# A two-stream encoder trunk: two more groups of input columns in the planned weave, new costs in its planner, and the first stream's attention over the columns that are left

## The chip, the core and the metric

The kernel runs on one core of a Trainium2 chip. TensorE (PE) multiplies, with its weight loads (PEld) beside the matmuls; VectorE (DVE) and ScalarE (ACT) do the elementwise work; GpSimd (POOL) does a few memsets; SyncE (SP) issues all DMAs. The metric is the device time of one execution in microseconds; lower is better.

## What is computed

Two requests of 512 tokens with 1024 channels go through the same two layers. Each layer is `x + rmsnorm(branch(rmsnorm(x)))`.

- Layer 0, RWKV-7: projections r, k, v, z (1024 x 1024 each) of the token mixed with its neighbours, small two-stage projections for decay and learning rate, and then, per head of 64 channels and in both directions, the scan `S_t = S_(t-1) (diag(decay_t) + a_t b_t^T) + v_t k_t^T`, `y_t = S_t r_t`. The two directions are summed, normalised per head, given a bonus term, gated with silu(z) and projected by w_o.
- Layer 1, neighbourhood attention: a projection w_in of 1024 x 4096 gives q, k, v, z; 16 heads attend on an 8 x 64 grid of tokens, each token to a window of 8 rows x 16 columns with a learned bias; the output is gated with silu(z) and projected by w_ao.

Everything is float32. A large product is made as three fast products: each operand is split into a rounded part hi (a cast on ACT) and the rest lo (a subtraction on DVE), and hi·hi, hi·lo and lo·hi are summed.

## The kernel before, in words

**Stages.** A prelude (stream 0 and 1: norms, mixing, first columns) runs to about 172 us. Then comes the *weave* (`scan_phase`, line 1585, and `weave`, line 1553), to 1172 us. It holds the scan of both streams, all that prepares and finishes it, and a stream of 76 columns. A column is a piece of a weight matrix of 1024 x 128; its product with the operands of one stream is 24 matmuls of 128 x 128 by 512. Then `rest` (line 1685) runs the attention of stream 0 beside the columns left over (to 1345 us), its output projection `out1(0)`, and the same for stream 1.

**The weave's order is written out by a planner.** Each piece of work is a generator (`Thread`, line 190) that yields the engine of its next operations, a gate, and a time from which its inputs are there. `Clock` (line 51) keeps a modelled time for each engine and each tile: `one` (line 112) gives each emitted instruction a cost on its engine, and what reads its result may start after that cost plus the engine's latency in `LAT`. `weave` picks, again and again, an open thread whose time has come: work for other engines ahead of work for PE, and then the lowest rank. On an engine other than PE nothing is emitted that would start later than its inputs by more than `EPS` (60 ns), or further ahead of PE's time than `AHEADE` (200 ns for ACT and DVE). The instructions of PE, DVE and ACT then stand on their engines in just this order. The ranks: the scan's steps 0, its helpers 0.5 to 1, `preps` 1.5, evacuation of columns (`posts`) 2, operands 2.5, splits of weights 3 or 9, `finish` 4, `inverse` 5, products 9.

**The scan** goes over 8 blocks (two streams x four groups of four heads) of 8 steps. `preps` (917) makes a block's factors. `inverse` (922) inverts 32 triangles per partition with thirty pairs of DVE operations, each reading what the one before wrote (lines 941 and 942), and then some transposes and small products. `step` (1080) passes through PE, ACT, PE, ACT, PE and DVE, where the new state S is an addition (1165) and a multiplication (1166). `finish` (1180) normalises a block's output.

**The columns** (`stream`, 1510; `flow`, 681) come in groups with common operands: nine groups, r, v, k, r, v, z, w_o of stream 0, the last two of z, and w_in of stream 0, of which the weave takes `4 * NPA` = 20 columns. `loads` brings weights on SP, at most three halves ahead (`NRAW`), `splits` splits them, `fetched` brings operand tiles, `operands` splits those into pairs of `act` buffers (18 in all, nine pairs), `products` multiplies.

The last group's operands are the residual x1 = x + h·post0·rstd, times pre1. In `x1n` (1518) and `operands` one thread makes each of the eight tiles k as six operations in turn: scale on DVE (1526), add on DVE (1529), hi on ACT (728), lo on DVE (733), square on ACT (1534), sum on DVE (1538). h is fetched to one of three `xr` buffers, x to a spare `act` or `vs` buffer.

**Attention of stream 0** (`rest`): for each of the last 8 - NPA = 3 groups p of w_in its four columns (`inproj`, 1318, 32 steps a group), then the eight columns of w_o of stream 1 (`out0`, 1264, 64 steps). Beside them the heads run (`heads`, 1348; 16 units for each of eight pairs of heads): `run(g, (a, n))` emits n units per step of g.

```python
for p in range(self.NPA, NP):
    run(self.inproj(0, self.xa, p), (a, self.POST0))
    queue.append(self.heads(0, p))
run(self.out0(1), (a, self.POST))
while queue:
    next(a)
```

With POST0 0.7 and POST 1.0. This stage is ordered by the tile framework's own scheduler, not by `Clock`.

Of the kernel before, what the change touches and what calls it, by code (L numbers as in the profile page):

```python
# [19 lines left out]
P = 128  # L20
T = 512
# [29 lines left out]
class Clock:  # L51
# [1 line left out]


    ENG = {"PE": "P", "Activation": "A", "DVE": "D", "Pool": "G", "SP": "S"}
    LAT = dict(P=200.0, A=45.0, D=45.0, G=90.0, S=0.0)
    BANKS = ("pf", "zy", "us", "pm", "pg", "pt", "po")

    def __init__(self, nc):
# [52 lines left out]
    def one(self, e, i):  # L112
        ap = lambda xs: [x for x in xs if hasattr(x, "bass_ap")]
        outs, ins = ap(i.outs), ap(i.ins)
        if not outs:
            return 0.0
        name = lambda x: x.bass_ap.tensor.name
        t = issued = self.t[e]
        for table, xs in ((self.made, ins), (self.used, outs)):
            for x in xs:  # L120
                for f, at in table.get(name(x), {}).items():
                    if f != e or e == "S":
                        t = max(t, at)
        free = lambda x: int(np.prod([n for _, n in x.ap[1:]])) if len(x.ap) > 1 else 1
        n = max([free(outs[0])] + [free(x) for x in ins[:1]])
        if e == "P":
            t, done = self.matmul(i, ins, free(outs[0]), t)
        elif e == "S":

            self.t[e] = issued = max(issued, self.t["P"]) + 380.0  # L130
            size = outs[0].ap[0][1] * free(outs[0]) * 4
            c = size * 0.0027 + 150.0
            self.dq = max(issued + 800.0, self.dq) + c
            done = max(self.dq, t + 800.0 + c) + 670.0
        else:
            if e == "A":
                c = 175.0 + 0.86 * n
            elif e == "G":
                c = 150.0 + n
            else:  # L140
                kind = type(i).__name__
                sb = [x for x in ins if free(x) > 8 and not name(x).startswith(self.BANKS)]
                c = 80.0 + 1.06 * n
                if "Reciprocal" in kind:
                    c = 80.0 + 6.2 * n
                elif getattr(i, "is_tensor_tensor_scan", False):
                    c = 80.0 + 2.1 * n
                elif "Transpose" in kind:
                    c = 80.0 + 1.8 * n
                elif len(sb) == 1 and len(ins) <= 2 and "TensorTensor" not in kind and "Reduce" not in kind and free(outs[0]) == n:  # L150
                    c = 110.0 + 0.53 * n if not getattr(i, "is_scalar_tensor_tensor", False) else 130.0 + 1.06 * n
            self.t[e] = t + c
            done = t + c + self.LAT[e]
        for x in ins:
            u = self.used.setdefault(name(x), {})
            u[e] = max(u.get(e, 0.0), done)
            self.slot[name(x)] = True
        for x in outs:
            for table in (self.used, self.made):
# [54 lines left out]

class Trunk:
    NACT, NW, NRAW, NXR, NTMP, WP = 18, 4, 3, 3, 5, 512
    POST0, POST, POST2, POST3, NPA = 0.7, 1.0, 0.15, 0.66, 5
    HP, HS = (1000, 0), 1000
    OUT1 = ("pg", "pg", "pg", "pg")
    HPA = 1000  # L220
# [13 lines left out]
    CH, FIRST, WFIRST = 100, 17, 3  # L234
    NVS = 2
    NZ1, STOCK, EPS, NEAR = 6, 1, 60.0, 400.0
    AHEADE = dict(S=3000.0, A=200.0, D=200.0)

    def __init__(self, ctx, tc, a):
# [441 lines left out]
    def flow(self):  # L681
# [2 lines left out]
        nc, did, ck = self.nc, self.did, self.clock  # L684
        cols = [(g, j, src, done) for g, (_, _, c) in enumerate(self.groups) for j, (src, done) in enumerate(c)]
        name = lambda *xs: [x.tensor.name for x in xs]
        raw, w, x, todo = {}, {}, {}, {}
        self.xq, self.post = x, {}
        for k, t in enumerate(self.groups[0][1]):
# [19 lines left out]
        def fetched():  # L709
            for g, (ready, source, _) in enumerate(self.groups):  # L710
                for k in range(KT if g else 0):
                    yield "S", lambda: ready() and 8 * g + k < min(did["x"] + self.NACT // 2 + self.NXR - 1, 8 * len(self.groups) - 8 + did["x1"] + self.NXR)
                    todo[g, k] = source(k)

        def operands():
            for g in range(1, len(self.groups)):
                for k in range(KT):
                    yield "S", lambda: (g, k) in todo
                    src, before, by, then = todo.pop((g, k))
                    for e, f in before:  # L720
                        yield e, None, lambda c: c.at(name(src))
                        f()
                    yield "A", lambda: 8 * g + k < did["x"] + self.NACT // 2 - (by is not None), lambda c: c.at(name(src))
                    lo, hi = self.pair()
                    if by is None:
                        nc.scalar.copy(hi, src)
                    else:
                        nc.scalar.activation(hi, src, AF.Identity, scale=by)
                    yield "D"
                    if by is None:  # L730
                        nc.vector.tensor_tensor(lo, src, hi.bitcast(F32), op=ALU.subtract)  # L731
                    else:
                        nc.vector.scalar_tensor_tensor(lo, src, by, hi.bitcast(F32), op0=ALU.mult, op1=ALU.subtract)
                    x[g, k] = hi, lo
                    for e, f in then:
                        yield e
                        f()

        def products():
            free, room = self.bank()  # L740
# [18 lines left out]
        def posts(a):  # L759
# [5 lines left out]
        few = lambda: did["split"] - did["k"] // 4 <= self.STOCK  # L765
        return [
            Thread(lambda: 0, loads()), Thread(lambda: 3 if few() else 9, splits()), Thread(lambda: 0, fetched()), Thread(lambda: 2.5, operands()),
            Thread(lambda: 9, products()), Thread(lambda: 2, posts(0)), Thread(lambda: 2, posts(1))]


    def prep(self, s, p):
# [139 lines left out]
        ks = kps[0]  # L911
        yield "D"
        vt.tensor_tensor(ks, kps[0], kps[1], op=ALU.add)
        vt.scalar_tensor_tensor(ks, ks, self.vec("rk", p), r, op0=ALU.mult, op1=ALU.mult)
        self.save("ks", s, p, ks)

# [5 lines left out]
    def inverse(self, s, pb):  # L922
# [14 lines left out]
        for q in range(1, 31):  # L937
            n = 31 - q
            tv = tmp[:, :n * q].rearrange("p (i j) -> p i j", i=n)
            yield "D"  # L940
            vt.tensor_tensor(tv, N[:, q + 1:, q:q + 1].broadcast_to([P, n, q]), N[:, q:q + 1, :q].broadcast_to([P, n, q]), op=ALU.mult)  # L941
            vt.tensor_tensor(N[:, q + 1:, :q], tv, N[:, q + 1:, :q], op=ALU.add)  # L942
        yield "D"
        vt.tensor_tensor(N, N, self.lower, op=ALU.mult)
        vt.memset(N.rearrange("p i j -> p (i j)")[:, 0:1024:33], 1.0)

        yield "D"
# [132 lines left out]
    def step(self, q):  # L1080
# [77 lines left out]
        if not st.last:  # L1158
# [4 lines left out]
                vt.tensor_tensor(st.S, so, wc, op=ALU.mult)  # L1163
            else:
                vt.tensor_tensor(st.S, so, before.S, op=ALU.add)
                vt.tensor_tensor(st.S, st.S, wc, op=ALU.mult)

        yi = st.y[:, min(st.i, 7 - st.i)]
# [11 lines left out]
    def finish(self, s, pb, y):  # L1180
# [14 lines left out]
        bc = lambda t: t.unsqueeze(2).broadcast_to([P, 16, HD])  # L1195
        yield "D", None, need(y)
        vt.tensor_reduce(st[:, 0], yv, axis=AX.X, op=ALU.add)
        vt.tensor_scalar(st[:, 1], st[:, 0], -1.0 / HD, None, op0=ALU.mult)
        yield "D"
        vt.tensor_tensor(yv, yv, bc(st[:, 1]), op=ALU.add)  # L1200
# [71 lines left out]
    def norm0(self, s):  # L1272

        nc = self.nc
        if s == 0:
# [1 line left out]
            self.x1_acc = self.t("vs", bufs=self.NVS)  # L1277
            yield from self.rstds(self.h_acc)
            self.made.add(("hr", s))
            yield "P", lambda: self.did["x1"] == KT, lambda c: c.at([self.x1_acc.tensor.name])  # L1280
            yield from self.rstds(self.x1_acc)
            self.x1_rstd = self.x1_acc
            self.made.add(("x1", s))
# [226 lines left out]
    def stream(self):  # L1510
# [1 line left out]
        sp = self.sp  # L1512
        cols = lambda s, kind, ps=range(NP): [
            (self.a["w_" + kind][p], lambda ps, p=p: self.column(s, kind, p, ps)) for p in ps]
        disk = lambda kind, s: lambda k: (self.load(self.t("xr", bufs=self.NXR), sp[kind, s, k]), [], None, [])
        vt, act = self.nc.vector, self.nc.scalar

        def x1n(k):

            h = self.load(self.t("xr", bufs=self.NXR), sp["h", 0, k])  # L1520
            x = self.t("act", (P, T), self.NACT, F32R).bitcast(F32) if k % 3 else self.t("vs", bufs=self.NVS)
            self.load(x, self.a["xc"][0][k * P:(k + 1) * P, :])
            sq = []

            def scaled():
                vt.scalar_tensor_tensor(h, h, self.vec("post0", k), self.h_acc, op0=ALU.mult, op1=ALU.mult)

            def added():
                vt.tensor_tensor(h, h, x, op=ALU.add)
                self.save("x1", 0, k, h)  # L1530

            def squared():
                sq.append(self.tmp() if k else self.x1_acc)
                act.activation(sq[0], h, AF.Square)

            def summed():
                if k:
                    vt.tensor_tensor(self.x1_acc, sq[0], self.x1_acc, op=ALU.add)
                self.did["x1"] += 1

            return h, [("D", scaled), ("D", added)], self.vec("pre1", k), [("A", squared), ("D", summed)]

        now = lambda: True
        groups = [
# [310 lines left out]
```

## Time and profile before

| | us |
|---|---|
| median of 3 runs | 1693.5 (1692.28 to 1696.38) |
| the profiled execution | 1695.69, of it the span 1693.9 |
| PE busy | 1542.3 (91%) |
| DVE busy | 1243.6 (73%) |
| ACT busy | 987.9 (58%) |
| mean granted clock of PE | 0.958 |
| the weave, 172 to 1172 | PE busy 879.4 of 1000 |
| attention of stream 0, 1172 to 1345 | PE busy 173.0 of 173 |

A row of a group reads: line, engine, operation, out<-in, partitions x elements, count | busy us, mean ns of one | idle time of the engine just before them, and who ended it. A row in order of time reads: start, duration, engine, line, and in brackets the idle time before and who ended it. A row of stretches reads: from:to, length, busy us (and instructions) of PE, PEld, DVE, ACT and POOL, the granted clock, the DMA's share and its GB/s; asked for one line, it has only that line's engines.

### The profile page before, as it was taken

The page shows a single profiled execution, that of the slowest core. Times are in us where ns is not written, and L with a number is a line of the kernel's source. Part 1 is how long each engine was busy: PE and PEld are TensorE (multiplying, and loading weights), DVE is VectorE, ACT ScalarE, POOL GpSimd, SP SyncE. Part 2 cuts the span into 40 slices and gives each one's busy share as a digit, 9 for nine tenths or more (in the row PEclk, how much of TensorE's full clock was granted, in tenths as well). Part 3 has the DMA queues.
Part 4 walks back from the last instruction along what each step waited for, and adds up shares of the span by engine and source line. Part 5 has one row for each costly group of instructions (what it writes and reads, how often), then busy time and mean ns, then how long its engine had stood idle before and what let it go on. Part 6 is the DMA issues. An engine that isn't in the chain of part 4 may idle for free.

```text
span 1693.9 us, 45876 instructions
## 1 busy us (share of the span) xinstructions
PE 1542.3 (91%) x18624; PEld 1171.7 (69%) x18624; DVE 1243.6 (73%) x2725; ACT 987.9 (58%) x1979; POOL 24.1 (1%) x94
## 2 busy tenths in 40 slices
PE   7989788889998988889978689999999999999998
PEld 6767556666676766666656477777777887777776
DVE  8985679688786886897878988656566686555564
ACT  5443655767665666667576545544567765555562
POOL 0000000000000000000000000000000000000000
PEclk9989989899999999999989799999999999999999
DMA  5435687786686777885667754557555346545553
GB/s 207 162 124 187 201 286 222 209 257 224 196 258 197 233 230 220 273 262 188 210 226 233 225 181 141 158 169 261 177 184 181 113 138 240 188 155 174 168 175 106
DMA packets 240819, 336.23 MB, mean 198 GB/s; under 512 B 53696, under 2 KB 119360, under 8 KB 240608
## 3 DMA queue, kind: packets, MB, share of 16 engines
q1 hardware_dynamic: 240608, 333.31, 61.2%
q8 instruction: 146, 2.39, 0.6%
q14 instruction: 65, 0.53, 0.1%
HBM read 227.71 MB, written 105.51 MB: 197 GB/s over the span
## 4 chain that ended last, share of the span: by engine, by line
PE 59%; DVE 16%; DMA 9%; ACT 9%; issue 5%; SPq 1%; DVEq 0%; ACTq 0%
PE pg L406 6%; PE pg L407 6%; PE pg L408 6%; PE pm L751 5%; PE pm L752 4%; PE pm L753 4%; PE sc L1375 2%; PE pf L1035 2%; PE po L1408 2%; DVE etmp L941 2%; DVE N L942 2%; PE pt L1393 1%; PE zy L1106 1%; DVE wlo L705 1%; PE us L1133 1%
## 5 line engine op out<-in xcount | busy, mean ns | idle before, releaser
L751 PE MATMUL pm<-act,whi 128*128 128x512 f32 x608 | 272.5, 448 | 19.4 <-ACT whi L703 8.9
L753 PE MATMUL pm<-act,wlo 128*128 128x512 f32 x608 | 249.2, 410 | 13.3 <-DVE wlo L705 11.9
L752 PE MATMUL pm<-act,whi 128*128 128x512 f32 x608 | 248.6, 409 | 11.2 <-DVE act L731 8.3
L406 PE MATMUL pg<-act,whi 128*128 128x512 f32 x480 | 199.8, 417 | 0.0
L407 PE MATMUL pg<-act,whi 128*128 128x512 f32 x480 | 190.2, 396 | 0.0
L408 PE MATMUL pg<-act,wlo 128*128 128x512 f32 x480 | 189.8, 396 | 0.0
L355 ACT CAST whi<-raw 128x512 fp32r<-128x512 f32 x156 | 96.4, 619 | 134.8 <-PE pg L407 87.9
L751 PEld LDWEIGHTS pm<-act,whi 128*128 128x128 f32 x608 | 119.2, 196 | 60.5 <-issue 13.3
L753 PEld LDWEIGHTS pm<-act,wlo 128*128 128x128 f32 x608 | 119.3, 196 | 50.0 <-DVE wlo L705 19.4
L356 DVE TENSOR_TENSOR wlo<-raw,whi 128x512 fp32r<-128x512 f32 x156 | 106.7, 686 | 59.8 <-ACT whi L355 49.8
L752 PEld LDWEIGHTS pm<-act,whi 128*128 128x128 f32 x608 | 119.7, 197 | 34.8 <-DVE act L731 11.4
L705 DVE TENSOR_TENSOR wlo<-raw,whi 128x512 fp32r<-128x512 f32 x152 | 103.3, 684 | 46.8 <-ACT whi L703 43.7
L703 ACT CAST whi<-raw 128x512 fp32r<-128x512 f32 x152 | 93.1, 618 | 31.4 <-PE pm L752 13.1
L408 PEld LDWEIGHTS pg<-act,wlo 128*128 128x128 f32 x480 | 90.7, 189 | 19.9 <-issue 0.7
L406 PEld LDWEIGHTS pg<-act,whi 128*128 128x128 f32 x480 | 90.9, 189 | 19.4 <-issue 4.8
L407 PEld LDWEIGHTS pg<-act,whi 128*128 128x128 f32 x480 | 91.0, 190 | 17.2 <-issue 3.0
L942 DVE TENSOR_TENSOR N<-etmp,N 128x30 f32<-128x30 f32 (+14 forms) x240 | 79.7, 332 | 8.2
L941 DVE TENSOR_TENSOR etmp<-N 128x30 f32<-128x30 f32 (+14 forms) x240 | 78.4, 327 | 4.5
L1386 DVE CUSTOM_DVE_ANT_0 sb<-sc,bias 128x256 f32<-128x256 f32 x128 | 50.5, 420 | 39.8 <-PE pt L1393 29.2
L1389 ACT ACTIVATE sb<-sb,mx 128x256 f32<-128x256 f32 x128 | 64.2, 503 | 16.4 <-DVE mx L1388 16.0
L1035 PE MATMUL pf<-cab 64*64 64x128 f32 (+1 forms) x2048 | 69.9, 274 | 3.7 <-issue 3.1
L1145 ACT COPY X<-us 64x256 f32<-64x256 f32 x128 | 46.8, 366 | 33.7 <-PE zy L1013 31.2
(381 smaller groups left out, 3298.3 us busy)
## 6 DMA issues: line engine op xcount, KB each, us to landing
dab<-ab SPq DMA_DIRECT2D x32, 1024.0 KB, 7.3
cab<-dab SPq DMA_DIRECT2D x64, 512.0 KB, 4.3
raw<-in_w_in_dram SPq DMA_DIRECT2D x128, 256.0 KB, 3.4
bias<-in_rpb_dram SPq DMA_DIRECT2D x32, 384.0 KB, 4.1
raw<-in_w_z_dram SPq DMA_DIRECT2D x32, 256.0 KB, 5.3
dz<-tmp SPq DMA_DIRECT2D x32, 256.0 KB, 3.3
raw<-in_w_k_dram SPq DMA_DIRECT2D x32, 256.0 KB, 2.6
dk<-tmp SPq DMA_DIRECT2D x32, 256.0 KB, 3.1
```

Of the source, the lines that this page charges most:

```text
L355: self.nc.scalar.copy(hi, src)
L356: (eng or self.nc.vector).tensor_tensor(lo, src, hi.bitcast(F32), op=ALU.subtract)
L406: nc.tensor.matmul(ps, hi, x[k][0], start=(k == 0), stop=False)
L407: nc.tensor.matmul(ps, hi, x[k][1], start=False, stop=False)
L408: nc.tensor.matmul(ps, lo, x[k][0], start=False, stop=(k == KT - 1))
L705: nc.vector.tensor_tensor(lo, raw.pop(h), hi.bitcast(F32), op=ALU.subtract)
L751: nc.tensor.matmul(ps, hi[:, at], xh, start=(k == 0), stop=False)
L752: nc.tensor.matmul(ps, hi[:, at], xl, start=False, stop=False)
L753: nc.tensor.matmul(ps, lo[:, at], xh, start=False, stop=(k == KT - 1))
L941: vt.tensor_tensor(tv, N[:, q + 1:, q:q + 1].broadcast_to([P, n, q]), N[:, q:q + 1, :q].broadcast_to([P, n, q]), op=ALU.mult)
L942: vt.tensor_tensor(N[:, q + 1:, :q], tv, N[:, q + 1:, :q], op=ALU.add)
L1035: end = nc.tensor.matmul(st.f[half(a), h, 0, d, g] if st.last else st.f[half(a), h, :, d, g], ab[half(h), d, g, 2 * e[d] + 1 - a], rt if s ...
```

## The change

1. `NPA` goes from 5 to 7: the weave takes 28 columns of w_in, the attention stretch one group of w_in and the eight columns of w_o. `POST0` goes to 1.0 and `POST` to 1.32.
2. The planner's costs: latencies 210, 125, 116 and 120 ns for PE, ACT, DVE and POOL (200, 45, 45, 90 before); ACT 85 + 0.85 n ns (175 + 0.86 n), DVE 82 + 1.02 n (80 + 1.06 n). On ACT and DVE an operation that reads what the same engine wrote now waits for the latency too.
3. The residual is made by three threads of rank 0.6, `residual`, `scaled` and `squares`, instead of within `operands`. `held` counts the `act` buffers in use; the h tiles of k = 3 and 4 (`HACT`) are fetched to `act` buffers. The norm of x1 waits for the last sum (`x1s`).
4. Five more yields between two DVE operations of one thread: in `prep`, `inverse` (twice), `step`, `finish`, so that other work may be put between them.

```diff
-    LAT = dict(P=200.0, A=45.0, D=45.0, G=90.0, S=0.0)
+    LAT = dict(P=210.0, A=125.0, D=116.0, G=120.0, S=0.0)
...
-                    if f != e or e == "S":
+                    if f != e or e == "S" or e in "AD" and table is self.made:
...
-                c = 175.0 + 0.86 * n
+                c = 85.0 + 0.85 * n
...
-                c = 80.0 + 1.06 * n
+                c = 82.0 + 1.02 * n
...
-    POST0, POST, POST2, POST3, NPA = 0.7, 1.0, 0.15, 0.66, 5
+    POST0, POST, POST2, POST3, NPA = 1.0, 1.32, 0.15, 0.66, 7
...
+    HACT = (3, 4)
...
-                    yield "S", lambda: ready() and 8 * g + k < min(did["x"] + self.NACT // 2 + self.NXR - 1, 8 * len(self.groups) - 8 + did["x1"] + self.NXR)
+                    if g < len(self.groups) - 1:
+                        yield "S", lambda: ready() and 8 * g + k < did["x"] + self.NACT // 2 + self.NXR - 1
+                    else:
+                        yield "S", lambda: ready() and k < did["x1"] + 5 and held() + (k in self.HACT) + (k % 3 > 0) <= self.NACT
                     todo[g, k] = source(k)
 
+        def held():
+            return 2 * (8 + did["pair"] - did["x"]) + did["act"]
...
+        def residual():
+            for k in range(KT):
+                yield "S", lambda: (last, k) in todo
+                h, xc = todo[last, k]
+                yield "D", None, lambda c: c.at(name(h))
+                nc.vector.scalar_tensor_tensor(h, h, self.vec("post0", k), self.h_acc, op0=ALU.mult, op1=ALU.mult)
+                yield "D", None, lambda c: c.at(name(h, xc))
+                nc.vector.tensor_tensor(h, h, xc, op=ALU.add)
+                self.save("x1", 0, k, h)
+                did["act"] -= k % 3 > 0
+                did["sum"] += 1
+
+        def scaled():
+            for k in range(KT):
+                yield "S", lambda: did["sum"] > k
+                h = todo[last, k][0]
+                yield "A", lambda: held() + 2 <= self.NACT, lambda c: c.at(name(h))
+                lo, hi = self.pair()
+                did["pair"] += 1
+                nc.scalar.activation(hi, h, AF.Identity, scale=self.vec("pre1", k))
+                yield "D"
+                nc.vector.scalar_tensor_tensor(lo, h, self.vec("pre1", k), hi.bitcast(F32), op0=ALU.mult, op1=ALU.subtract)
+                x[last, k] = hi, lo
+
+        def squares():
+            for k in range(KT):
+                yield "S", lambda: (last, k) in x
+                h = todo.pop((last, k))[0]
+                yield "A", None, lambda c: c.at(name(h))
+                sq = self.tmp() if k else self.x1_acc
+                nc.scalar.activation(sq, h, AF.Square)
+                did["act"] -= k in self.HACT
+                did["x1"] += 1
+                if k:
+                    yield "D"
+                    nc.vector.tensor_tensor(self.x1_acc, sq, self.x1_acc, op=ALU.add)
+                did["x1s"] += 1
...
+            Thread(lambda: 0.6, residual()), Thread(lambda: 0.6, scaled()), Thread(lambda: 0.6, squares()),
...
             vt.tensor_tensor(tv, N[:, q + 1:, q:q + 1].broadcast_to([P, n, q]), N[:, q:q + 1, :q].broadcast_to([P, n, q]), op=ALU.mult)
+            yield "D"
             vt.tensor_tensor(N[:, q + 1:, :q], tv, N[:, q + 1:, :q], op=ALU.add)
...
                 vt.tensor_tensor(st.S, so, before.S, op=ALU.add)
+                yield "D"
                 vt.tensor_tensor(st.S, st.S, wc, op=ALU.mult)
```

More of the change, by code (lines that the diff above doesn't have):

```diff
@@ L686, in flow @@
         name = lambda *xs: [x.tensor.name for x in xs]
+        last = len(self.groups) - 1
         raw, w, x, todo = {}, {}, {}, {}
@@ L713, in fetched @@
                     todo[g, k] = source(k)
+        def held():
+            return 2 * (8 + did["pair"] - did["x"]) + did["act"]
         def operands():
-            for g in range(1, len(self.groups)):
+            for g in range(1, len(self.groups) - 1):
                 for k in range(KT):
                     yield "S", lambda: (g, k) in todo
[L719 to L723, printed above, removed]
+                    src = todo.pop((g, k))
+                    yield "A", lambda: 8 * g + k < did["x"] + self.NACT // 2, lambda c: c.at(name(src))
@@ L724, in operands @@
                     lo, hi = self.pair()
[L725 to L728, printed above, removed]
+                    did["pair"] += 1
+                    nc.scalar.copy(hi, src)
                     yield "D"
[L730 to L733, printed above, removed]
+                    nc.vector.tensor_tensor(lo, src, hi.bitcast(F32), op=ALU.subtract)
@@ L734, in operands @@
                     x[g, k] = hi, lo
-                    for e, f in then:
-                        yield e
-                        f()
+        def residual():
[9 more added lines that the diff above has]
+                did["sum"] += 1
@@ new lines, in scaled @@
+        def scaled():
[4 more added lines that the diff above has]
+                lo, hi = self.pair()
+                did["pair"] += 1
+                nc.scalar.activation(hi, h, AF.Identity, scale=self.vec("pre1", k))
+                yield "D"
+                nc.vector.scalar_tensor_tensor(lo, h, self.vec("pre1", k), hi.bitcast(F32), op0=ALU.mult, op1=ALU.subtract)
+                x[last, k] = hi, lo
@@ L944, in inverse @@
         vt.tensor_tensor(N, N, self.lower, op=ALU.mult)
+        yield "D"
         vt.memset(N.rearrange("p i j -> p (i j)")[:, 0:1024:33], 1.0)
@@ L1165, in step @@
                 vt.tensor_tensor(st.S, so, before.S, op=ALU.add)
+                yield "D"
                 vt.tensor_tensor(st.S, st.S, wc, op=ALU.mult)
@@ L1197, in finish @@
         vt.tensor_reduce(st[:, 0], yv, axis=AX.X, op=ALU.add)
+        yield "D"
         vt.tensor_scalar(st[:, 1], st[:, 0], -1.0 / HD, None, op0=ALU.mult)
@@ L1279, in norm0 @@
             self.made.add(("hr", s))
-            yield "P", lambda: self.did["x1"] == KT, lambda c: c.at([self.x1_acc.tensor.name])
+            yield "P", lambda: self.did["x1s"] == KT, lambda c: c.at([self.x1_acc.tensor.name])
             yield from self.rstds(self.x1_acc)
@@ L1514, in stream @@
             (self.a["w_" + kind][p], lambda ps, p=p: self.column(s, kind, p, ps)) for p in ps]
-        disk = lambda kind, s: lambda k: (self.load(self.t("xr", bufs=self.NXR), sp[kind, s, k]), [], None, [])
+        disk = lambda kind, s: lambda k: self.load(self.t("xr", bufs=self.NXR), sp[kind, s, k])
         vt, act = self.nc.vector, self.nc.scalar
         def x1n(k):
-            h = self.load(self.t("xr", bufs=self.NXR), sp["h", 0, k])
-            x = self.t("act", (P, T), self.NACT, F32R).bitcast(F32) if k % 3 else self.t("vs", bufs=self.NVS)
+            act = lambda: self.t("act", (P, T), self.NACT, F32R).bitcast(F32)
+            h = act() if k in self.HACT else self.t("xr", bufs=self.NXR)
+            self.load(h, sp["h", 0, k])
+            x = act() if k % 3 else self.t("vs", bufs=self.NVS)
             self.load(x, self.a["xc"][0][k * P:(k + 1) * P, :])
[L1523 to L1541, printed above, removed]
+            self.did["act"] += (k in self.HACT) + (k % 3 > 0)
+            return h, x
         now = lambda: True
```

## The prediction

> **What bounds the kernel now.** I read the page first, for the whole span.
>
> ```profile
> span 1693.9 us, 45876 instructions
> ...
> PE 1542.3 (91%) x18624; PEld 1171.7 (69%) x18624; DVE 1243.6 (73%) x2725; ACT 987.9 (58%) x1979; POOL 24.1 (1%) x94
> ```
>
> PE is busy 91% of the span, an average over stages. So I asked next for the busy time of each engine by stretch (stretch, length, busy us of PE, PEld, DVE, ACT and POOL, granted clock, DMA share, GB/s): the weave, its middle, the piece where the first stream's residual is made, the weave's end, and the first stream's attention.
>
> ```profile
> 172.00:1172.00 1000.00, 879.44 (x15156) 655.57 (x15157) 784.92 (x1497) 613.21 (x1193) 22.27 (x50) 0.94 0.69 219
> 340.00:840.00 500.00, 448.53 (x8468) 329.79 (x8467) 411.55 (x798) 320.65 (x639) 9.62 (x26) 0.97 0.73 230
> 840.00:1000.00 160.00, 128.89 (x2050) 95.91 (x2050) 134.30 (x237) 103.07 (x191) 2.46 (x7) 0.85 0.67 216
> 1145.00:1172.00 27.00, 27.00 (x125) 21.56 (x124) 14.93 (x32) 11.06 (x18) 0.00 (x0) 1.00 0.82 285
> 1172.00:1345.00 173.00, 173.00 (x1065) 135.18 (x1064) 112.55 (x399) 113.15 (x264) 0.00 (x0) 1.00 0.53 174
> ```
>
> See three things. The attention stretch has no idle PE at all, and DVE and ACT stand at 65% there: it is bound by PE. The weave has 1000 - 879.4 = 120.6 us of idle PE. And the weave's end, from 1145 us on, is nothing but columns at full PE: the scan is over by then, and columns are still left. So **a microsecond of idle PE taken away anywhere in the weave comes off its end**, and that is the only place where much can be won.
>
> What ends the idle time? The groups of the weave, by line (busy us, mean ns | idle before, releasers):
>
> ```profile
> L751 PE MATMUL pm<-act,whi 128*128 128x512 f32 x607 | 272.1, 448 | 19.4 <-ACT whi L703 8.9 <-issue 4.6 <-ACT act L728 4.0
> L753 PE MATMUL pm<-act,wlo 128*128 128x512 f32 x606 | 248.4, 410 | 13.3 <-DVE wlo L705 11.9 <-issue 1.3
> L752 PE MATMUL pm<-act,whi 128*128 128x512 f32 x607 | 248.3, 409 | 11.2 <-DVE act L731 8.3 <-issue 2.3 <-DVE act L733 0.4
> L942 DVE TENSOR_TENSOR N<-etmp,N 128x30 f32<-128x30 f32 (+14 forms) x240 | 79.7, 332 | 8.2
> L941 DVE TENSOR_TENSOR etmp<-N 128x30 f32<-128x30 f32 (+14 forms) x240 | 78.4, 327 | 4.5
> L1165 DVE TENSOR_TENSOR S<-us,S 128x256 f32<-128x256 f32 x48 | 20.1, 419 | 13.4 <-PE us L1153 8.4 <-ACT whi L703 3.2 <-issue 0.6
> ```
>
> Products of columns account for 19.4 + 13.3 + 11.2 = 43.9 us, and of that 8.9 + 4.0 + 11.9 + 8.3 + 0.4 = 33.5 us is PE standing at a product whose split operand is late. PE takes its instructions in the order that the planner wrote, so each such stop is a place where the planner thought ACT or DVE would be done and they were not.
>
> **The change part by part.**
>
> *Eight columns moved.* Groups 5 and 6 of w_in leave the attention stretch and join the weave's end. Each column is 24 matmuls, 2 loads of weights and a save on SP, 2 splits on ACT and 2 on DVE, and the evacuation (one DVE and one or two ACT operations, one more DVE for z). The 27 us from 1145 on hold 125 matmuls, 0.216 us each, so a column costs 24 x 0.216 = 5.2 us and eight cost 41.5 us, in a place that is PE-bound; they leave a place that is PE-bound too. Net: **0**. Bounds: 41.5 us gained, if the weave would otherwise have run out of columns before the scan ends (it does not: 27 us of columns are left over), and 3 us lost, if the longer dense end runs at the 90% of the middle for part of its length. The sixteen loads stay behind the same limit of three raw buffers; the heads' first loads of bias, q, k, v now follow them on SP, later by as much as PE is.
>
> *The residual in three threads.* Today one thread makes each of the eight tiles of the last operand group in turn: scale, add, hi, lo, square, sum, alternately on DVE and ACT, at rank 2.5.
>
> ```profile
> L1526 DVE SCALAR_TENSOR_TENSOR xr<-xr,cv,acc x8: 739/744/746, 886.1 to 959.4; 128x512 f32<-128x512 f32 x8
> 900.00:960.00 60.00, 4.77 (x9) 1.88 (x9) 0.91 0.77 244
> ```
>
> Eight tiles are spread over 886 to 959 us, 10 us apiece, and in 60 us of that (second row: line 751 alone, from the stretches) only nine products' first matmuls run, against 284 in the 500 us of the middle. So PE starves. The new threads run at rank 0.6, and the residual need not wait for operand buffers, only the hi/lo pairs do (gate `held`; two of the h tiles sit in operand buffers instead of the three xr). Idle PE in 840 to 1000 us is 160 - 128.9 = 31.1 us; at the middle's share, 51.5 of 500, it would be 16.5. Bound of the gain: 14.6 us. But DVE is busy 134.3 of these 160 us, and the residual's rank takes it from the preparation and the inverse, so I take **-9**; the lower end is 0.
>
> *The granted clock there.* It is 0.85 in this stretch and 0.97 in the middle. The profile shows how it gets there:
>
> ```profile
> 939.00 0.40 PE L753 MATMUL pm<-act,wlo 128*128 128x512 f32 x1
> ...
> 955.30 0.80 PE L751 MATMUL pm<-act,whi 128*128 128x512 f32 x1 [3.99 <-ACT act L728]
> ```
>
> The same matmul takes 0.40 us in the busy part and 0.80 behind a 4 us hole. The whole deficit against the middle, (0.97 - 0.85) x 128.9 = 15 us, is the bound; shorter holes give part of it: **-4**.
>
> *The planner's costs.* Do the new numbers fit the chip better? Rows of DVE in order of time (start, duration):
>
> ```profile
> 612.30 0.32 DVE L941 TENSOR_TENSOR etmp<-N 128x168 f32<-128x168 f32 x1
> 612.65 0.33 DVE L942 TENSOR_TENSOR N<-etmp,N 128x168 f32<-128x168 f32 x1
> 612.90 0.74 DVE L1230 SCALAR_TENSOR_TENSOR bv<-pm,dv,bv 128x512 f32<-128x512 f32 x1
> 613.68 0.75 DVE L1232 SCALAR_TENSOR_TENSOR bv<-bv,dv,sz 128x512 f32<-128x512 f32 x1
> ```
>
> and of two splits on ACT, and DVE's next start behind a 512-wide split:
>
> ```profile
> 600.28 1.14 ACT L703 CAST whi<-raw 128x512 fp32r<-128x512 f32 x2
> ...
> 605.43 0.62 ACT L703 CAST whi<-raw 128x512 fp32r<-128x512 f32 x1 [0.20 <-DMA raw<-in_w_v_dram]
> ```
>
> ```profile
> 623.27 0.71 DVE L705 TENSOR_TENSOR wlo<-raw,whi 128x512 fp32r<-128x512 f32 x1
> 623.88 1.93 DVE L954 STREAM_TRANSPOSE MT<-N 128x1024 f32<-128x1024 f32 x1
> ```
>
> L942 reads what L941 wrote and starts 0.35 us behind it; L1230 reads nothing of L942 and starts 0.25 us behind it. So a dependent start costs 0.10 us more, which the old planner leaves out on one engine and the new one sets at 0.116. Two splits on ACT take 1.14 us where one takes 0.62: they start 0.52 us apart, and the new 85 + 0.85 x 512 = 520 ns meets that while the old 615 does not; DVE's next start is 0.61 us on, new 604, old 623. The new costs are nearer in all three. The bound of what that can give is the 33.5 us above, less 4.4 already counted with the residual (L728, L733): 29 us. A third of it, **-10**, since the plan's DMA model stays as it is; the other end is a plan that fits better and changes nothing, or one whose longer hops delay the scan: +10.
>
> *More yields.* DVE may now put other work between two dependent operations. That frees at most 480 x 0.10 = 48 us of DVE time, but DVE has 215 us to spare in the weave, so of PE time I count only -3. Against it: the pair L1165, L1166 of the scan's state is on the chain of every step, and a 0.6 us operation may slip between; 48 pairs x 0.6 = 29 us at most, covered by columns on PE: +3. Together **0**. [...]
>
> *Attention over fewer columns.* Each head is 16 units, 128 in all. Before: 96 steps x 0.7 + 64 x 1.0 = 131, all heads done inside the columns. After: 32 x 1.0 + 64 x 1.32 = 116, so the last twelve units come behind the columns. At 173/131 = 1.32 us a unit they would cost 16 us alone; the next projection's first columns (seven of eight operand tiles are ready) can fill PE for most of it: +3, bounds 0 and +16. Within the stretch, the length falls to 173 - 41.5 = 131 us if PE still sets it. DVE: 112.6 less eight columns x (2 x 0.69 + 0.69 + 0.17 for z) = 18 leaves 95 of 131, 72%; ACT about the same. PE now has no idle; at the weave's shares of DVE (78%) it has 12%, so part of that appears: +3, bounds 0 and +42 (below). Together **+6**.
>
> Sum: 0 - 9 - 4 - 10 + 0 + 6 = **-17 us** on the profiled execution's 1695.7 us (span 1693.9 and 1.8 around it), 1678.7. The median of the three runs, 1693.5, is 2.2 lower; against it the forecast is 1676.5.
>
> **The rivals.**
>
> *Attention becomes its own bound (slower).* The softmax units, two matrices of 128 x 256 per head and block of queries:
>
> ```profile
> L1386 DVE CUSTOM_DVE_ANT_0 sb<-sc,bias 128x256 f32<-128x256 f32 x60 | 24.1, 420 | 18.7 <-PE pt L1393 12.3 <-PE sc L1375 5.2
> L1391 DVE TENSOR_SCALAR sb<-sb,mx 128x256 f32<-128x256 f32 x64 | 22.3, 352 | 1.4
> L1390 DVE RECIPROCAL mx<-mx 128x1 f32<-128x1 f32 x64 | 9.9, 160 | 7.0 <-ACT sb L1389 6.5
> L1389 ACT ACTIVATE sb<-sb,mx 128x256 f32<-128x256 f32 x63 | 31.6, 503 | 11.7 <-DVE mx L1388 11.5
> ```
>
> 64 units in 173 us is 2.7 us each; afterwards 131/64 = 2.05. One unit's chain is 0.42 + 0.15 + 0.50 + 0.16 + 0.35 = 1.6 us without its hops (0.15 is the negation of the maximum, about as long as the reciprocal), and the scores have one buffer. If the pace cannot fall below 2.5 us, the stretch lasts 160 us: with the tail +32 instead of +6, and -23 + 32 = +9, **about 1703** against the median. It decides from 2.35 us a unit on, where the 20 us lost and the tail eat the weave's 23. For it: DVE waited 12.3 us for PE's transposes already. Against: DVE and ACT are at 65%.
>
> *The scan's blocks get longer (slower).*
>
> ```profile
> 544.22 2.05 DVE L934 STREAM_TRANSPOSE N<-Gd 128x1024 f32<-128x1024 f32 x1
> 620.09 2.10 DVE L949 STREAM_TRANSPOSE NA<-N 128x1024 f32<-128x1024 f32 x1
> 657.50 1.97 DVE L934 STREAM_TRANSPOSE N<-Gd 128x1024 f32<-128x1024 f32 x1
> ```
>
> One inverse follows the next, 113 us a block, and 76 us pass over sixty short operations of some 20 us: at rank 5 they get what is left of DVE. Twice the yields is twice the chances to be passed over. What is left over at the end, 27 us, and the 41.5 us of moved columns cover 68 us of a later scan, some 10 us a block over seven blocks; it decides from 12 us a block on. At 15, the scan ends 105 us later and 36 are not covered: -23 + 6 + 36 = +19, **about 1713**.
>
> *The new plan gives most of its bound (faster):* -25 from late operands, -14 from the residual, -10 clock, +4 attention: -45, **1649**.
>
> *It does not do what it says:* the order changes, the stalls only move, within 5 us of **1693**.
>
> **How the numbers follow.** Forecast 0.38; large gain 0.20; attention bound 0.22; longer blocks 0.12; no effect 0.08. Within 0.3% (5 us) is what measurement cannot tell from no change: same 0.08. Faster 0.58, slower 0.34. Both signs hold much, so the range goes from 1640 to 1714; the forecast's own is 1666 to 1688.
>
> **What would show it.** Right: idle PE in the weave under 105 us against 120.6, the eight L1526-type operations within 40 us instead of 73, late-operand idle before the three product lines near 20 us, the weave's end near 1172 + 41 - 23 = 1190 us, and the attention stretch near 137 us with PE above 95%. Wrong: that stretch over 150 us, L934 more than 120 us apart, or the product lines' idle unchanged.

## The result and the profile after

The changed kernel takes 1702.84 us (median of 5, 1701.14 to 1704.07) against 1696.3 before on the same chip (5 runs): ratio 1.0049, 95% interval 1.0026 to 1.0073. It is slower by half a per cent; the forecast was 1% faster. The profiled execution took 1704.07 us.

The first line of the page of the kernel after (its span is 1702.3 us), and the stretches that answer to those of before (stretch, length, busy us of PE, PEld, DVE, ACT, POOL, granted clock, DMA share, GB/s): the weave, its middle, the residual's piece, attention up to the end of its columns, and its tail.

```profile
PE 1559.3 (92%) x18624; PEld 1185.7 (70%) x18624; DVE 1228.7 (72%) x2725; ACT 985.2 (58%) x1979; POOL 24.1 (1%) x94
```

```profile
172.00:1213.00 1041.00, 936.61 (x15347) 702.62 (x15346) 786.22 (x1523) 625.59 (x1214) 22.26 (x50) 0.92 0.68 216
340.00:840.00 500.00, 456.14 (x8198) 337.41 (x8196) 389.44 (x769) 317.21 (x627) 9.62 (x26) 0.91 0.70 221
840.00:1000.00 160.00, 137.79 (x2305) 104.98 (x2305) 136.66 (x260) 98.70 (x190) 2.46 (x7) 0.86 0.68 221
1213.00:1345.00 132.00, 132.00 (x882) 103.99 (x881) 93.38 (x367) 96.02 (x236) 0.00 (x0) 1.00 0.55 180
1345.00:1360.00 15.00, 6.98 (x37) 4.04 (x36) 14.69 (x30) 8.48 (x19) 0.00 (x0) 0.78 0.35 107
```

PE, DVE and ACT do the same work in the same number of instructions as before, and PE is busy 17 us longer. The weave's idle PE fell nearly as forecast, to 1041 - 936.6 = 104.4 us from 120.6. But its busy PE rose by 936.6 - 879.4 = 57.2 us, 41.5 for the moved columns, by the prediction's estimate, and **15.7 beyond them, which I put down to a lower granted clock**, 0.92 against 0.94 in all and 0.91 against 0.97 in the middle. The weave thus gained next to nothing: it is 40 us longer, for 41.5 us of columns. Attention lost 10 us: up to the last head's output, the stretch fell by 31 us, from 172 (1172.4 to 1344.4) to 141 (1212.8 to 1354.0), not by 41.5. The 8 us of idle PE lie behind the last column, 1345 to 1360, where DVE is busy 14.7 of 15 us. Together +8.4 us of span.

The product lines of the weave (busy us, mean ns | idle before, releasers) and the residual's first operation (ns, first to last start; the two tiles in operand buffers lie between):

```profile
L786 PE MATMUL pm<-act,whi 128*128 128x512 f32 x671 | 306.4, 457 | 28.8 <-ACT whi L705 9.6 <-ACT act L731 8.8 <-ACT act L755 6.7
L787 PE MATMUL pm<-act,whi 128*128 128x512 f32 x670 | 276.7, 413 | 13.4 <-DVE act L733 13.1 <-DVE act L757 0.3
L788 PE MATMUL pm<-act,wlo 128*128 128x512 f32 x670 | 274.5, 410 | 6.7 <-DVE wlo L707 6.7
```

```profile
L741 DVE SCALAR_TENSOR_TENSOR xr<-xr,cv,acc x6: 743/746/747, 885.4 to 924.3; 128x512 f32<-128x512 f32 x6
```

The late operands did not go: 45.2 us of named releasers against 33.5. PE waits less for the weights' lo halves (6.7 against 11.9), more for operand tiles (act: 28.9 against 12.7). The residual did go faster, 39 us against 73.

How a late operand costs twice is seen on PE in order of time:

```profile
756.89 0.40 PE L788 MATMUL pm<-act,wlo 128*128 128x512 f32 x1
758.57 0.50 PE L786 MATMUL pm<-act,whi 128*128 128x512 f32 x1 [1.29 <-ACT act L731]
760.16 0.80 PE L787 MATMUL pm<-act,whi 128*128 128x512 f32 x1 [1.09 <-DVE act L733]
760.75 0.63 PE L788 MATMUL pm<-act,wlo 128*128 128x512 f32 x1
761.18 0.63 PE L856 MATMUL pm<-h,w2h 128*128 128x512 f32 x1
```

From 747 to 755 us such matmuls start 0.23 us apart. Behind the two holes, of 1.3 and 1.1 us, they start 0.43 us apart (760.75, 761.18), up to 764 us, although PE no longer waits.

### The profile page after: what moved, and what is told of

Same layout as the page of the kernel before. It is cut to its first block, busy times and chain, and to the rows that moved or that the text cites. A ratio compares the mean times of both kernels' runs of the same rounds, so it can differ in the third digit from the quotient of the medians.

```text
span 1702.3 us, 45902 instructions
## 1 busy us (share of the span) xinstructions
PE 1559.3 (92%) x18624; PEld 1185.7 (70%) x18624; DVE 1228.7 (72%) x2725; ACT 985.2 (58%) x1979; POOL 24.1 (1%) x94
## 4 chain that ended last, share of the span: by engine, by line
PE 44%; DVE 3%; ACT 3%; DMA 3%; issue 1%; DVEq 0%; SPq 0%; ACTq 0%
PE pg L407 5%; PE pg L408 5%; PE pg L409 5%; PE pm L786 4%; PE pm L787 3%; PE pm L788 3%; PE sc L1416 2%; PE po L1449 2%; PE pt L1434 1%; PE pf L1074 1%; PE us L1192 1%; PE us L1172 1%; PE zy L1145 1%; PE zy L1196 1%; DMA raw<-in_w_ao_dram 1%
## 5 line engine op out<-in xcount | busy, mean ns | idle before, releaser
L786 PE MATMUL pm<-act,whi 128*128 128x512 f32 x672 | 306.9, 457 | 28.8 <-ACT whi L705 9.6
L787 PE MATMUL pm<-act,whi 128*128 128x512 f32 x672 | 277.5, 413 | 13.4 <-DVE act L733 13.1
L788 PE MATMUL pm<-act,wlo 128*128 128x512 f32 x672 | 275.3, 410 | 6.7 <-DVE wlo L707 6.7
L786 PEld LDWEIGHTS pm<-act,whi 128*128 128x128 f32 x672 | 132.6, 197 | 81.9 <-issue 17.4
L407 PE MATMUL pg<-act,whi 128*128 128x512 f32 x416 | 172.2, 415 | 6.4 <-ACT act L356 6.4
L408 PE MATMUL pg<-act,whi 128*128 128x512 f32 x416 | 166.9, 401 | 0.7 <-DVE act L357 0.7
L409 PE MATMUL pg<-act,wlo 128*128 128x512 f32 x416 | 166.8, 401 | 0.0
L787 PEld LDWEIGHTS pm<-act,whi 128*128 128x128 f32 x672 | 133.9, 199 | 41.7 <-DVE act L733 18.2
L788 PEld LDWEIGHTS pm<-act,wlo 128*128 128x128 f32 x672 | 133.4, 199 | 38.7 <-DVE wlo L707 8.8
L705 ACT CAST whi<-raw 128x512 fp32r<-128x512 f32 x168 | 102.8, 617 | 75.0 <-PE pm L787 28.9
L407 PEld LDWEIGHTS pg<-act,whi 128*128 128x128 f32 x416 | 79.6, 192 | 24.3 <-ACT act L356 6.6
L408 PEld LDWEIGHTS pg<-act,whi 128*128 128x128 f32 x416 | 79.7, 192 | 17.3 <-issue 2.6
L409 PEld LDWEIGHTS pg<-act,wlo 128*128 128x128 f32 x416 | 79.5, 191 | 16.7 <-issue 0.7
L1097 DVE TENSOR_TENSOR AK<-zy,cc 128x256 f32<-128x256 f32 x63 | 26.6, 423 | 61.8 <-PE zy L1052 61.1
```

The costliest lines, as they stand in the source:

```text
L407: nc.tensor.matmul(ps, hi, x[k][0], start=(k == 0), stop=False)
L408: nc.tensor.matmul(ps, hi, x[k][1], start=False, stop=False)
L409: nc.tensor.matmul(ps, lo, x[k][0], start=False, stop=(k == KT - 1))
L705: nc.scalar.copy(hi, raw[h])
L786: nc.tensor.matmul(ps, hi[:, at], xh, start=(k == 0), stop=False)
L787: nc.tensor.matmul(ps, hi[:, at], xl, start=False, stop=False)
```

## The experiments

Ratios are to runs of the kernel before on the same chip, with their 95% intervals. The theory at first was *clock and tail*: less idle PE, but a lower clock, and attention's last units; the rivals put the loss on the moved columns, on the yields or on the residual's rank.

**The parts one by one.** (Of each edit some lines are shown; e4 is the third part of the change, as it stands above.) e1: the changed kernel with the stages of before; e2: with POST 1.5; e3: the kernel before with part 2 of the change alone; e4: with part 3 alone; e5: the changed kernel without part 4.

```diff
e1 -    POST0, POST, POST2, POST3, NPA = 1.0, 1.32, 0.15, 0.66, 7
e1 +    POST0, POST, POST2, POST3, NPA = 0.7, 1.0, 0.15, 0.66, 5
e2 +    POST0, POST, POST2, POST3, NPA = 1.0, 1.5, 0.15, 0.66, 7
e3 +    LAT = dict(P=210.0, A=125.0, D=116.0, G=120.0, S=0.0)
e3 +                    if f != e or e == "S" or e in "AD" and table is self.made:
e3 +                c = 85.0 + 0.85 * n
e3 +                c = 82.0 + 1.02 * n
e5 -            yield "D"
...
```

> The changed kernel with NPA 5, POST0 0.7 and POST 1.0, as before the change; costs, yields and residual threads stay. Theory (clock and tail): the weave is worth nothing, because 16 us less idle PE is eaten by a lower granted clock, and the other 8 us are the tail of attention; so the attention stretch is back at 173 us, and the total is that of the kernel before, 1691 to 1698 us, with a mean clock still near 0.945. Rival (staging): the moved columns are the whole loss and the new plan is a gain hidden behind it; then the total is under 1688 us.

> The changed kernel with POST 1.5 instead of 1.32, so that 32 x 1.0 + 64 x 1.5 = 128 units fit into the columns. Theory (tail): the 8 us of idle PE between 1345 and 1360 us are the twelve units behind the columns; they shrink to under 3 us and the total falls by 5 to 8 us, to 1695 to 1698. Rival (attention is its own bound): the units cannot go faster, idle PE appears within the stretch instead, and the total stays within 2 us of 1702.8.

> The kernel before with the planner's new costs and latencies alone. Theory (clock): from 340 to 840 us idle PE falls below 48 us against 51.5, but the granted clock falls from 0.97 to 0.93 or less, and the total is 1694 to 1706 us. Rival (the yields lower the clock, or the residual): the clock stays at 0.96 or more and the total falls by about 10 us, to 1684 to 1690.

> The kernel before with the three residual threads, the new fetch gate and the two h tiles in operand buffers alone. Theory (the residual is a gain of its own): the order up to about 880 us is the one before, clock 0.97 there; idle PE from 840 to 1000 us falls from 31 to about 22 us, and the total falls by 6 to 12 us, to 1684 to 1690. Rival (its rank takes DVE from the inverse and delays the scan by as much): the total is within 3 us of 1696, with the last state step of the scan later than 1132 us.

> The changed kernel without the five added yields. Theory (the new costs are the loss, the yields add to it): residual -18, costs +17 and staging -4, as the first four runs gave them, add up to -5, so the yields are the other 11 us; without them the total is 1688 to 1695 us and the granted clock from 340 to 840 us is about 0.93 instead of 0.91. Rival (the parts do not add up, the yields are nothing): 1700 to 1706.

| | us | ratio | clock, profiled |
|---|---|---|---|
| e1, stages back | 1706.95 | 1.0052 (1.0032 to 1.0072) | 0.947 |
| e2, POST 1.5 | 1702.82 | 1.0036 (1.0015 to 1.0057) | 0.945 |
| e3, new costs alone | 1713.5 | 1.0093 (1.0065 to 1.012) | 0.946 |
| e4, residual alone | 1678.02 | 0.9872 (0.9845 to 0.9899) | 0.964 |
| e5, without the yields | 1706.4 | 1.0079 (1.0049 to 1.0109) | 0.941 |

e1 missed: no 10 us come back. Its columns end at 1147 us, its scan at 1172, and PE is busy 18.9 us of the 25 between, so five groups were too few there. e2 missed too: all units are emitted within the columns, and neither the time nor the tail (8 us of idle PE, 1345 to 1360) changes. e3 puts 0.93% on the new costs, more than its theory allowed, and in the middle it shows what the theory said: idle PE 500 - 456.4 = 43.6 us, clock 0.93.

```profile
340.00:840.00 500.00, 456.44 (x8268) 335.50 (x8268) 399.93 (x771) 322.19 (x640) 9.63 (x26) 0.93 0.72 225
```

e4 seemed to put a gain of 1.3% on the residual, 18 us where at most 12 were expected, with the middle as before and the piece behind it better in idle PE (24 us against 31) and clock (0.94 against 0.85):

```profile
340.00:840.00 500.00, 449.99 (x8476) 330.95 (x8475) 413.52 (x800) 322.64 (x642) 9.62 (x26) 0.97 0.74 231
840.00:1000.00 160.00, 136.06 (x2125) 103.59 (x2124) 138.49 (x245) 106.19 (x198) 2.46 (x7) 0.94 0.73 237
```

e5 missed: the yields are worth nothing that can be told, since the intervals of 1.0079 here and 1.0049 of the changed kernel overlap.

**Which of the new costs.** e6: ACT's new numbers alone on the kernel before; e7: DVE's alone; e9: ACT's new cost with a latency of 220; e10: ACT's old cost with its new latency.

```diff
e6  +    LAT = dict(P=200.0, A=125.0, D=45.0, G=90.0, S=0.0)
e6  +                c = 85.0 + 0.85 * n
e7  +    LAT = dict(P=200.0, A=45.0, D=116.0, G=90.0, S=0.0)
e7  +                    if f != e or e == "S" or e == "D" and table is self.made:
e7  +                c = 82.0 + 1.02 * n
e9  +    LAT = dict(P=200.0, A=220.0, D=45.0, G=90.0, S=0.0)
e9  +                c = 85.0 + 0.85 * n
e10 +    LAT = dict(P=200.0, A=125.0, D=45.0, G=90.0, S=0.0)
```

> The kernel before with ACT's new cost and latency alone (85 + 0.85 n and 125 instead of 175 + 0.86 n and 45; the result of an operation of 512 is due after 645 ns instead of 660, and ACT is thought free after 520 instead of 615). Theory (ACT's shorter cost makes operands late): PE waits over 10 us for split operands of columns (act) from 340 to 840 us, against 2.5 on one line before, the clock there is 0.94 or less, the total 1702 or more. Rival (DVE's part does it): the total is within 5 us of 1696 and the clock is 0.96 or more.

> The kernel before with DVE's new cost, latency and same-engine wait alone (82 + 1.02 n and 116 instead of 80 + 1.06 n and 45). Theory (ACT's part is the loss): DVE's new numbers fit the rows and give a little, the total is 1688 to 1698 and the clock from 340 to 840 us is 0.96 or more. Rival (DVE's part does it, since a dependent operation now lets another thread in, and the scan and the inverse lose their turn): the last state step of the scan comes at 1150 us or later instead of 1132, the clock is 0.94 or less, the total 1702 or more.

> The kernel before with ACT's new cost (85 + 0.85 n) but a latency of 220, so that ACT is thought free after 520 ns (512 wide) while its result is due after 740, 80 later than before. Theory (the room is lost: with 95 ns less per operation the planner books ACT full, and what the plan does not know, DMA landings and table loads, has no slack left): slow all the same, 1702 or more, clock of the whole run 0.950 or less. Rival (the due time is what counts, the new one is 15 ns too early): within 5 us of the 1695 before.

> The kernel before with ACT's old cost (175 + 0.86 n) and its new latency 125, so that the result is due after 740 ns and ACT is thought busy for 615 as before. Theory (room): within 5 us of 1695 or a little faster, clock 0.955 or more. Rival (any other order than the tuned one is slower): 1702 or more.

e6 took 1709.02 us, 1.0084 (1.0058 to 1.011); e7 1694.17, 1.0007 (0.9985 to 1.0028); e9 1697.34, 1.0022 (1.0006 to 1.0038); e10 1725.49, 1.0183 (1.0151 to 1.0215). So ACT's numbers seemed to be the loss, by their room (how long the planner thinks ACT is busy) or their due times (when it expects the result), but e9 and e10 fit neither: the one with less room is nearly as before, the one with more room and a later due time is the slowest. In e6 the middle's idle PE is that of before, 50.6 against 51.5 us, operand tiles do not hold PE up for the 10 us that its theory said, and the clock alone is lower, 0.94:

```profile
340.00:840.00 500.00, 449.40 (x8269) 333.79 (x8262) 412.53 (x796) 319.19 (x633) 9.63 (x26) 0.94 0.73 226
```

e7 speaks against the middle's rows as a guide: idle PE falls to 45.7 us there and the clock to 0.92, and the median is the same. (Its profiled execution, 1702.46 us, is the slowest of its twelve.)

**The stages with the old costs.** e8: the residual, seven groups, POST 1.5; e12: the residual, four groups; e11: the residual with DVE's new numbers.

```diff
e8  +    POST0, POST, POST2, POST3, NPA = 1.0, 1.5, 0.15, 0.66, 7
e12 +    POST0, POST, POST2, POST3, NPA = 0.6, 0.9, 0.15, 0.66, 4
```

> The three residual threads with the old costs and no added yields, and seven groups of w_in in the weave with POST0 1.0 and POST 1.5. Theory (moving columns is worth nothing as long as columns are left when the scan ends): within 5 us of the 1678 of the residual alone, with the scan over at about 1136 us, columns to about 1200, and the attention stretch at 132 to 140 us. Rival (shorter attention costs its tail of 8 us): 1684 to 1690.

> The residual threads with old costs and four groups of w_in in the weave, POST0 0.6 and POST 0.9, so 128 units fit beside 24 columns. Theory (columns cost the same wherever PE is full, and attention needs enough of them beside it): the scan ends at 1136 us and the columns of the weave with it, attention's stretch is 21 us longer with PE full to its end, total within 4 us of 1678. Rival (each column more beside attention is a gain): 1674 or less.

> The residual threads with DVE's new cost, latency and same-engine wait, ACT's cost as before, no added yields, five groups. Theory (parts add up): the residual's 1678 within 5 us. Rival (DVE's numbers shift columns ahead of the scan, as the last state step at 1159 us instead of 1132 showed, and with the residual early the columns run out before the scan ends): 1684 or more, with PE idle at the weave's end.

e8: 1690.64 us, 0.9983 (0.9964 to 1.0003); e12: 1678.58, 0.9908 (0.9892 to 0.9925); e11: 1689.42, 0.9976 (0.9958 to 0.9993). From e4 to e8 the ratio rises by 1.1%, and in the profiles 11 us are lost by the end of `out1(0)` and 8 in all: the weave is 42.2 us longer, the columns' price, and attention only 29 us shorter. e8 after its 1201 us of weave, and e4 after its 1159:

```profile
1201.00:1320.00 119.00, 119.00 (x790) 94.51 (x789) 83.95 (x324) 85.48 (x210) 0.00 (x0) 1.00 0.57 181
1320.00:1350.00 30.00, 21.90 (x132) 16.05 (x132) 24.61 (x69) 19.50 (x44) 0.00 (x0) 0.83 0.31 95
```

```profile
1159.00:1327.00 168.00, 168.00 (x1052) 132.48 (x1050) 113.54 (x409) 112.77 (x265) 0.00 (x0) 1.00 0.59 195
```

With 12 columns beside eight pairs of heads, the columns run out before the heads do, although all units were emitted beside them; 8 us of idle PE and some slow clock remain. With 20 columns PE is full to the end, and 24 (e12) are no better. e11 shows no sum of parts: 0.9976 where e4 and e7 together would give 0.988.

**Is it the content or the order?** Four shifts of one planner number, by 2 to 10 ns, on the kernel before (e13 to e16), and two of them on the residual version (e17, e18). They change no operation; they change which one the planner puts first.

```diff
e13, e17 +    LAT = dict(P=200.0, A=50.0, D=45.0, G=90.0, S=0.0)
e14      +    LAT = dict(P=200.0, A=45.0, D=55.0, G=90.0, S=0.0)
e15, e18 +    LAT = dict(P=195.0, A=45.0, D=45.0, G=90.0, S=0.0)
e16      +    NZ1, STOCK, EPS, NEAR = 6, 1, 62.0, 400.0
```

> The kernel before with ACT's latency in the planner 50 instead of 45. Theory (order: another order than the tuned one costs by itself, whatever its reason): the total moves by 5 us or more, more likely up, 1698 to 1715. Rival (content: the new costs are bad numbers, and 5 ns are nothing): within 4 us of 1694.

> The kernel before with DVE's latency in the planner 55 instead of 45. Theory (order): 1698 to 1715. Rival (content): within 4 us of 1694.

> The kernel before with PE's latency in the planner 195 instead of 200. Theory (order): 1698 to 1715. Rival (content): within 4 us of 1694.

> The kernel before with the planner's tolerance EPS 62 instead of 60 ns. Theory (order): 1698 to 1715. Rival (content): within 4 us of 1694.

> The residual threads alone, with ACT's latency in the planner 50 instead of 45. Theory (the residual's gain is its own): 10 us or more under the kernel before with the same shift. Rival (one lucky order): within 5 us of that kernel.

> The residual threads alone, with PE's latency in the planner 195 instead of 200. Theory (own gain): 10 us or more under the kernel before with the same shift. Rival (one lucky order): within 5 us of that kernel.

| shift | on the kernel before | on the residual version |
|---|---|---|
| ACT 50 | e13: 1.0102 (1.0053 to 1.0151) | e17: 1.0122 (1.0072 to 1.0172) |
| DVE 55 | e14: 1.0107 (1.0064 to 1.015) | |
| PE 195 | e15: 1.0049 (1.0017 to 1.0081) | e18: 1.0048 (1.0026 to 1.007) |
| EPS 62 | e16: 1.012 (1.0084 to 1.0156) | |

That leaves the theories of content without support. A shift that says nothing new of the chip costs 0.5 to 1.2%, 8 to 20 us, as much as the new costs (e3, 0.93%); whether their content costs or gains something beside that, these runs cannot tell. And the gain of e4 belonged to one order: with the same shift on both sides it is nothing, and with DVE's new numbers on both sides (e11 against e7) it is 0.3%, with intervals that overlap. The weave of e13 (to its last column):

```profile
172.00:1196.00 1024.00, 894.09 (x15162) 665.32 (x15161) 787.51 (x1505) 612.03 (x1195) 22.26 (x50) 0.92 0.68 215
```

That of e17 is the same within 1.2 us of busy PE. Against the 1000 us of before, with its 120.6 us of idle PE at clock 0.94, they are 23 to 24 us longer: 9 to 10 of it idle PE and 13 to 15 busy PE at 0.92.

How fast the eight tiles of the residual follow one another depends on the order as well. e3 has no residual threads, e17 has them:

```profile
L1526 DVE SCALAR_TENSOR_TENSOR xr<-xr,cv,acc x8: 664/746/747, 885.2 to 929.2; 128x512 f32<-128x512 f32 x8
L741 DVE SCALAR_TENSOR_TENSOR xr<-xr,cv,acc x6: 728/744/745, 937.5 to 990.2; 128x512 f32<-128x512 f32 x6
```

The new costs without the threads take 44 us, the threads with the shift 53, and e13, that shift without the threads, 51. So the 39 us of the changed kernel are not the threads' doing alone.

## Why the prediction was wrong

- **The planner's costs (-10): this step failed.** It took the fit of three costs to the rows as a gain in time. The fit is real, but it brought no gain: alone the new costs read +0.93%, and shifts of 2 to 10 ns read +0.5 to +1.2%. What I had as the other end of that term, +10, is nearer to what came (e3: 17 us). It needs no longer hops to explain it: nine other orders of the same work on the kernel before (e3, e6, e7, e9, e10, e13 to e16) lie from 1.0007 to 1.0183, mean 1.0085, and none is clearly faster. The order of before is the best of ten; that it was chosen as such is likely but not shown.
- **The clock (-4):** the sign was wrong. In the residual's piece it hardly rose (0.85 to 0.86), and it fell in the middle, where I had left it out: busy PE +15.7 us in the weave. Idle PE fell by 16.2 us, near the 19 I had counted for it, and that was worth nothing. In part the match is luck: the late operands, from which 10 of the 19 were to come, rose by 11.7 us.
- **The residual (-9):** its rows came as predicted, 39 us instead of 73, and idle PE from 840 to 1000 us fell from 31 to 22. But e3 has 44 us without the threads, so the rows do not show the threads' share. As a gain of its own it is not shown: -1.3% in e4, nothing in e17 and e18.
- **Eight columns (0):** the price in the weave was right with the old costs (42.2 us for 41.5); with the new ones some of the bound on the gaining side came in, since in e1 the columns run out 25 us before the scan ends.
- **Attention (+6):** +10, mis-sized. The tail is not the twelve units behind the columns, since POST 1.5 does not move it (e2) or take it away (e8). What is left is the heads' own pace, with DVE busy 14.7 of the tail's 15 us; no run changes that pace by itself. Of the rivals, that was the first, at 141/64 = 2.2 us a unit, short of the 2.35 from which it decides. That its number, about 1703, is the measured one is luck: it has attention lose 32 us and the weave gain 23, and they lost 10 and gained next to nothing.
- **The scan's blocks:** the last state step came 42 us later, at 1173.7 us, which is this rival's direction, but less than the 68 us from which it decides, and the moved columns covered it.
- **The yields (0):** nothing can be told of them (e5). That is the scatter of orders, and it does not show the balance of -3 and +3 by which I came to 0.
- **The signs:** idle PE under 105 us, the residual within 40 us and an attention stretch near 137 us (141, PE above 95%) came; late operands near 20 us (45.2) and the weave's end near 1190 (1213) did not. The signs that came did not go with a gain.
- **The range and chances** were built from terms of this one plan. A term that only the runs showed, about 1% for another order, was missing, and in the nine orders tried it has a sign.

The theory of the clock holds as one way in which an order costs, beside idle PE (e13); it does not say why an order is a bad one. Open stays what makes an order good: neither the idle PE nor the fit of the costs tells it beforehand. e4 is faster than both kernels, and these runs show no reason for it that survives another order.

## What to carry to other kernels

Where a planner writes out the order, measure what a meaningless shift of its numbers does before crediting a change with less than that; here it is 0.5 to 1.2%. Repeat a gain under two such shifts on both sides: what does not survive belongs to the order. And count PE's idle time and its clock together, since what the one gives the other may take.

## What the runs showed of the hardware

The same program varies with the granted clock. Of the 23 runs of the kernel before beside e8, the fastest took 1682.92 us at a mean clock of 0.963, the slowest 1699.74 at 0.952; a fit over all of them gives 0.50 us of time for each us of (1 - clock) x time, correlation 0.77. The changed kernel's five runs lie at 0.941 to 0.947, on average 0.944 against 0.957 of those 23, so that (1 - clock) x time is 23 us more. By that slope this would be worth 11 us, more than the 6.5 by which it is slower. That is an estimate: the slope comes from runs of one program, and no run changes the clock alone.

The Trainium skill (TensorE: Matmul & The Clock Gate, section Part 1: The HAM clock gate) has PE drop to half rate after an idle window of some 3.4 us. The half rate is here, 0.43 us a matmul instead of 0.23, but the rows above show it behind holes of 1.3 and 1.1 us with one matmul between them: here idle time in pieces, 2.4 us together, was enough.
